# A norm weight that arrives as eight rows and is applied behind the transposes, and an inverse root computed on GpSimd

## The chip, the cores and the metric

The program runs on one core of one Trainium2 chip. A core has five engines with a queue of instructions each: TensorE (PE, with its weight loads listed as PEld), VectorE (DVE), ScalarE (ACT), GpSimd (POOL) and SyncE (SP), which here only starts DMAs. Data moves between HBM and the on-chip memory SBUF by 16 DMA engines; TensorE writes into a second on-chip memory, PSUM, which VectorE and ScalarE can read. The metric is the device time of one execution in microseconds (us); lower is better. Rows with SPq, POOLq or PEq show a queue's own work, such as the issue of a DMA.

## The reference, cut to what matters

All tensors are float32; there are 256 tokens of width 1024. The work is two transformer layers after one another:

```
# first layer
h = rms_norm(x, norm_mix);  z = h @ w_in          # 1024 -> 2560: gated unit, differential attention
x = x + concat(sgu(z), diff_attention(z)) @ w_out
x = x + memory_attention(rms_norm(x, norm_xq), rms_norm(mem, norm_mem), ...)
x = x + hierarchical_moe(rms_norm(x, norm_ffn), ...)   # 32 experts, 2 per token
x = rms_norm(x, norm_final)
# second layer
u = moba_attention(rms_norm(x, norm_mix_pre), w_qkv, w_o)     # 8 heads, all 256 tokens in one block
x = x + rms_norm(u, norm_mix_post)
u = square(relu(rms_norm(x, norm_ffn_pre) @ w_up)) @ w_down   # 1024 -> 4096 -> 1024
out = x + rms_norm(u, norm_ffn_post)

def rms_norm(x, g):
    return x * rsqrt(mean(x * x) + 1e-6) * g       # mean over the 1024 columns of a token
```

Two places matter. The first is the first norm: `norm_mix` is a weight per column, the inverse root a number per token. The second is the border of the layers: the final norm of the first layer and the first norm of the second follow each other, so for each token two inverse roots are needed, `r4[:, 0:2]` for the final norm of the two blocks of 128 tokens and `r4[:, 2:4]` for the norm behind it.

## The kernel before, in words

Matrix products are made nearly exact in float32 by splitting each operand into two parts of a faster 32-bit type, a high part (`hi`, `xh`, `whi`) and the rest (`lo`, `xl`, `wlo`), and adding three products: high with high, high with low, low with high (`mm3`, lines 177 to 179). A weight matrix comes in pieces of 512 columns (`Chunk`, line 102): four quarters of 128x1024 numbers each in `raw` tiles, started on SyncE's queue. For each quarter ScalarE makes the high part (line 129, `whi`) and VectorE subtracts it from the raw numbers for the low part (line 137, `wlo`, an instruction that reads two SBUF tiles). `whi` and `wlo` have six buffers each, `raw` has six of 1 MB.

The start is written out by hand in `first_mixers`, in a `manual_schedule` block: each engine runs its instructions in the order of the code. Before the first product TensorE multiplies the identity with itself (`keep_warm`, line 409: eleven times at first, eight times later), which computes nothing that is used. `norm_mix` is read from HBM 128 times over, once per partition, into a 512 KB tile `gmix` in one of the two buffers named `gb`. VectorE multiplies x by it (lines 424 and 429, one line for each block of 128 tokens), TensorE turns the result (line 387), ScalarE copies the turned block from PSUM as the high part (line 389) and VectorE takes the low part from PSUM (line 394). `project` (line 400) then multiplies by the first 512 columns of `w_in`. The inverse root of the norm is left out of all this and applied later. The `gb` buffers go round: an integer table in `setup` (line 314, read by the VectorE cast of line 318), then `gmix`, then `gmem` (`norm_mem`, line 419), then `norm_xq` (line 217, started on GpSimd's queue).

At the border of the layers (end of `moe`, lines 1292 to 1315) the products with the second layer's weights have already begun: the norms' inverse roots are applied behind the products. `vs` collects four columns, two per block of tokens (lines 1309 to 1312). `rsqrt(k, vs, 4)` makes `r4` with a chain of eight VectorE instructions of four columns (lines 67 and 87 to 94). Here Tile's scheduler orders the instructions, and it has put splits (`wlo`) between the links of this chain. `r4` is wanted by VectorE (`x`, line 1433), by ScalarE for the attention values (line 1455) and by TensorE, which turns it into a row (line 1445); VectorE copies that row to `rb` (line 1446) and scales the queries and keys of the first two heads by it (`by_token`, line 1449), after which TensorE computes their scores (lines 1469 and 1470). On GpSimd the product `gmg` of two weights (line 1505) waits for its second weight's DMA (line 217, `norm_ffn_pre`).

Of the kernel before, what the change touches and what calls it, by code (L numbers as in the profile page):

```python
# [9 lines left out]
F32 = mybir.dt.float32  # L10
# [4 lines left out]
AF = mybir.ActivationFunctionType  # L15
OP = mybir.AluOpType
# [38 lines left out]
def bcast_rows(ap, n):  # L55

    return bass.AP(tensor=ap.tensor, offset=ap.offset, ap=[[0, 128], [1, n]])
# [5 lines left out]
def rsqrt(k, v, n, scale=None):  # L63

    nc = k.nc
    seed = small(k, n, "rqi", dt=I32)
    nc.vector.tensor_scalar(seed, v.bitcast(I32), -0.5, MAGIC, op0=OP.mult, op1=OP.add)
    r0 = seed.bitcast(F32)
    y, w, u = small(k, n, "rqy"), small(k, n, "rqw"), small(k, n, "rqu")
    r = small(k, n, "rqr", 6)  # L70
    if n == 1:
        nc.vector.scalar_tensor_tensor(y, r0, v, r0, op0=OP.mult, op1=OP.mult)
        nc.vector.tensor_scalar(w, y, -1.0, None, op0=OP.add)
        nc.vector.tensor_scalar(u, y, C4, C3 - C4, op0=OP.mult, op1=OP.add)
        t = small(k, 1, "rqt")
        nc.vector.tensor_scalar(t, u, w, C2, op0=OP.mult, op1=OP.add)
        rw = small(k, 1, "rqx")
        if scale is not None:
            rs = small(k, 1, "rqs")
            nc.vector.tensor_mul(rs, r0, scale)  # L80
            r0 = rs
        nc.vector.tensor_mul(rw, r0, w)
        t2 = small(k, 1, "rqt")
        nc.vector.tensor_scalar(t2, t, w, C1, op0=OP.mult, op1=OP.add)
        nc.vector.tensor_scalar(r, t2, rw, r0, op0=OP.mult, op1=OP.add)
        return r
    nc.vector.tensor_mul(y, r0, r0)
    nc.vector.tensor_mul(y, y, v)
    nc.vector.tensor_scalar(w, y, -1.0, None, op0=OP.add)
    nc.vector.tensor_scalar(u, w, C4, C3, op0=OP.mult, op1=OP.add)  # L90
    nc.vector.tensor_mul(u, u, w)
    nc.vector.scalar_tensor_tensor(u, u, C2, w, op0=OP.add, op1=OP.mult)
    nc.vector.scalar_tensor_tensor(u, u, C1, w, op0=OP.add, op1=OP.mult)
    nc.vector.scalar_tensor_tensor(r, u, 1.0, r0, op0=OP.add, op1=OP.mult)
    return r
# [55 lines left out]
def cols(w, c0):  # L151

    return w[:, c0:c0 + 512].rearrange("(kt p) n -> p kt n", p=128)
# [12 lines left out]
def tok(tb):  # L166
    return slice(tb * 128, tb * 128 + 128)


def half(n):  # L170
    return slice(n * 512, n * 512 + 512)
# [49 lines left out]
def small(k, n, name, bufs=4, dt=F32):  # L221
    return k.sm.tile([128, n], dt, name=name if n <= 2 else name + "8", bufs=bufs if n <= 2 else 2)
# [80 lines left out]
def setup(k, const):  # L303
    nc, I = k.nc, k.I
    x = k.new_x().rearrange("p (t n) -> p t n", t=2)
    k.x = x

    ident = const.tile([128, 128], F32, name="ident")
    nc.gpsimd.memset(ident, 1.0)
    nc.gpsimd.affine_select(ident, ident, pattern=[[-1, 128]], compare_op=OP.is_equal, fill=0.0,  # L310
                            base=0, channel_multiplier=1)
    k.ident = ident

    di = k.pa.tile([128, 384], I32, name="gb", bufs=2)
    nc.gpsimd.iota(di[:, 0:128], pattern=[[1, 128]], base=0, channel_multiplier=-1)
    nc.gpsimd.iota(di[:, 128:384], pattern=[[1, 256]], base=-128, channel_multiplier=-1)
    dn = const.tile([128, 384], F32, name="dn")
    nc.vector.tensor_copy(dn, di)
    for c0 in (0, 256):
        nc.gpsimd.affine_select(dn[:, c0:c0 + 128], dn[:, c0:c0 + 128], pattern=[[-1, 128]],  # L320
                                compare_op=OP.is_ge, fill=NEG, base=0, channel_multiplier=1)
    k.dn = dn
# [23 lines left out]
def first_mixers(k):  # L346

    nc, tc, I = k.nc, k.tc, k.I
    x = k.x
    with ExitStack() as ctx:  # L350
        pb = ctx.enter_context(tc.tile_pool(name="pb", bufs=1))
# [15 lines left out]

        wi = I["w_in"][0]
        hT = new_T(k, 0)
        y = k.pa.tile([128, 2, 1024], F32, name="big8", bufs=1)  # L370
        gmix = k.pa.tile([128, 1024], F32, name="gb", bufs=2)
        nc.sync.dma_start(x[:, 0], I["x"][0, tok(0), :])
        nc.sync.dma_start(gmix, bcast_rows(I["norm_mix"], 1024))
        c = Chunk(k, cols(wi, 512), split=False,
                  between=lambda i: i or nc.sync.dma_start(x[:, 1], I["x"][0, tok(1), :]))
        c1, c2 = (Chunk(k, cols(wi, n), split=False) for n in (1024, 1536))
# [2 lines left out]
        xh, xl = hT  # L379
# [3 lines left out]
        def turned(tb, n):  # L383

            pt = k.wk.tile([128, 4, 128], F32, name="wk")
            for j in range(4):
                nc.tensor.transpose(pt[:, j], y[:, tb, tok(4 * n + j)], k.ident)
            d = (slice(None), slice(4 * n, 4 * n + 4), tok(tb))
            nc.scalar.activation(xh[d], pt, AF.Copy)
            return d, pt  # L390

        def lows(todo):
            for d, pt in todo:
                nc.vector.tensor_sub(xl[d], pt, xh[d].bitcast(F32))

        def project(tb, units, passes):

# [8 lines left out]
        def keep_warm(n):  # L406

            for i in range(n):
                nc.tensor.matmul(warm, k.ident, k.ident, start=True, stop=True)
# [9 lines left out]
        nc.sync.dma_start(gmem, bcast_rows(I["norm_mem"], 1024))  # L419
        with tc.manual_schedule(engines={nc.tensor.engine, nc.scalar.engine, nc.vector.engine,  # L420
                                         nc.gpsimd.engine}):
            keep_warm(11)
            for n in range(2):
                nc.vector.tensor_mul(y[:, 0, half(n)], x[:, 0, half(n)], gmix[:, half(n)])
            todo = [turned(0, n) for n in range(2)]
            c.high()
            lows(todo)
            for n in range(2):
                nc.vector.tensor_mul(y[:, 1, half(n)], x[:, 1, half(n)], gmix[:, half(n)])
            keep_warm(8)  # L430
            project(0, range(2), (0, 2))
            c.low(nc.vector)
# [1 line left out]
            todo = [turned(1, n) for n in range(2)]  # L434
# [46 lines left out]
            for i in range(8):  # L481
                tb, g = divmod(i, 4)
# [80 lines left out]
        for i in range(8):  # L563
            tb, g = divmod(i, 4)
# [47 lines left out]
        for qb in range(2):  # L612
            o = t2([128, 4, 128])
# [27 lines left out]
        for qb in range(2):  # L641
            o = os[qb]
            nc.vector.tensor_mul(o, o, ro[:, qb * 4:qb * 4 + 4, None].to_broadcast([128, 4, 128]))
            pt = k.wk.tile([128, 4, 128], F32, name="wk")
# [14 lines left out]
        y, parts = project_add(k, (mh, ml), I["w_out"][0], gxq)  # L659
# [273 lines left out]
def moe(k, oT):  # L933
# [3 lines left out]
    nc, tc, I = k.nc, k.tc, k.I  # L937
    x = k.x
    wg, wu, wd = I["w_gate"][0], I["w_up"][0], I["w_down"][0]
    R = Routing()  # L940
    with ExitStack() as ctx:
# [9 lines left out]
        y = R.raw2.tile([128, 2048], F32, name="raw").rearrange("p (t n) -> p t n", t=2)  # L951
# [157 lines left out]
        def keep_warm(tb, n):  # L1109

            for i in range(n):
                nc.tensor.matmul(macc[tb][0][:, 0:128], k.ident, k.ident, start=True, stop=True)
# [8 lines left out]
        pool = nc.gpsimd  # L1121
# [156 lines left out]
        with tc.manual_schedule(engines=order_of):  # L1278
            for p in range(SPILL, NP - 2):
                if p == GAINS:  # L1280
                    gains.extend(load_gain(k, name, nc.sync) for name in ("norm_final", "norm_mix_pre_2"))
                pair(p)
            gf, g1 = gains
            pool.tensor_tensor(g1, g1, gf, op=OP.mult)
            last_pairs()
            hT = new_T(k, 0)
            scatter(*pend, last=True)
            gained_T(k, R, macc, gains[1], hT, ahead[0])
            for i in range(2):
                ahead[1].high()  # L1290
                ahead[1].low()
            first = token_major(k, hT, ahead[0], range(8), pool=k.wk)
            x = k.x = k.new_x().rearrange("p (t n) -> p t n", t=2)
            y = k.pa.tile([128, 2, 1024], F32, name="big8", bufs=1)
            vs = small(k, 4, "vs")
            for tb in range(2):
                px, py = [], []
                for n in range(2):
                    xs, ys = x[:, tb, half(n)], y[:, tb, half(n)]
                    nc.vector.tensor_mul(ys, macc[tb][n], gf[:, half(n)])  # L1300
                    px.append(mean_sq(k, macc[tb][n], xs))
                    if n == 0:
                        py.append(mean_sq(k, ys, xs))
                    else:
                        py.append(small(k, 1, "ms", 8))
                        nc.vector.scalar_tensor_tensor(xs, ys, 1.0 / 1024, ys, op0=OP.mult, op1=OP.mult,
                                                       accum_out=py[n])
                v1, v2 = vs[:, tb:tb + 1], vs[:, 2 + tb:3 + tb]
                nc.vector.tensor_scalar(v1, px[0], px[1], RMS_EPS, op0=OP.add, op1=OP.add)
                my = small(k, 1, "my")  # L1310
                nc.vector.tensor_add(my, py[0], py[1])
                nc.vector.tensor_scalar(v2, v1, RMS_EPS, my, op0=OP.mult, op1=OP.add)
                ahead[1].high()
                ahead[1].low(nc.vector)
            r4 = rsqrt(k, vs, 4)
    return hT, ahead, first, y, r4


# [401 lines left out]
```

## Time and profile before

| | us |
|---|---|
| median of 3 runs (990.01 to 991.66) | 991.53 |
| the profiled execution, its time | 991.24 |
| its span, first to last instruction | 989.3 |
| TensorE busy in the span | 937.9 (95%) |
| VectorE busy | 450.0 (45%) |
| ScalarE busy | 329.2 (33%) |
| GpSimd busy | 39.8 (4%) |

The span is what the rows show; 1.94 us of the execution's time lie around it. The granted TensorE clock was 0.992 of full speed on average. TensorE is nearly always busy, but not everywhere on work that sets the end: between about 240 and 684 us, in the experts' stage, the weights stream in at some 420 GB/s and TensorE waits for them here and there. A busy share therefore says little; which wait ends last, stage by stage, says more.

### The profile page before, as it was taken

Reading aid. Unit: us, or ns where it says so; the run is one execution under the profiler, and the core shown is the slowest. Engines: PE = TensorE matmul, PEld = TensorE weight load, DVE = VectorE, ACT = ScalarE, POOL = GpSimd, SP = SyncE. Lnnn points to the kernel's source line nnn. Section 1 sums busy time; section 2 is a strip of 40 time slices with the busy share of each in tenths; the row PEclk is TensorE's granted clock in tenths of the full one; section 3 lists DMA queues with packets and bytes.
Section 4 is the critical chain, followed back from the end, with each engine's and each line's share of the span. In section 5 each row is a group of like instructions: output and inputs, shape, how many; then the busy total and the mean of one; then the engine's idle time right before and its main releaser. Section 6 shows DMA issues by size and latency. Waiting matters only on the chain. (4 is left out here: it accounts for less than half of the span.)

```text
span 989.3 us, 13343 instructions
## 1 busy us (share of the span) xinstructions
PE 937.9 (95%) x5308; PEld 650.5 (66%) x5308; DVE 450.0 (45%) x852; ACT 329.2 (33%) x518; POOL 39.8 (4%) x41
## 2 busy tenths in 40 slices
PE   8999999999999999999989999898999999999996
PEld 7988899874344444444334444334889879999995
DVE  6798775653221211111121211015875687555554
ACT  6657555531110110111111101103554455445541
POOL 0030000230000000000000000000120000000000
PEclk9999999999999999999999999999999999999999
DMA  9955464697999999999999999999845346655501
GB/s 355 353 205 177 140 211 137 201 348 279 401 426 421 424 421 424 425 422 424 423 420 413 421 424 422 423 424 400 291 149 171 128 152 196 205 174 196 185 1 43
DMA packets 86576, 293.23 MB, mean 296 GB/s; under 512 B 7088, under 2 KB 15824, under 8 KB 73712
## 3 DMA queue, kind: packets, MB, share of 16 engines
q1 hardware_dynamic: 85616, 289.56, 75.7%
q0 software_dynamic: 896, 2.79, 0.8%
q8 instruction: 43, 0.70, 0.3%
q14 instruction: 21, 0.17, 0.0%
HBM read 291.28 MB, written 1.05 MB: 295 GB/s over the span
## 5 line engine op out<-in xcount | busy, mean ns | idle before, releaser
L137 DVE TENSOR_TENSOR wlo<-raw,whi 128x1024 fp32r<-128x1024 f32 x156 | 189.0, 1222 | 100.4 <-ACT whi L129 99.4
L129 ACT ACTIVATE whi<-raw 128x1024 fp32r<-128x1024 f32 x156 | 163.0, 1057 | 143.7 <-PE acc L179 59.7
L1236 DVE COPY usb<-wk 128x512 f32<-128x512 f32 x16 | 11.0, 689 | 201.9 <-PE wk L1074 183.6
L177 PE MATMUL acc<-hTh,whi 128*128 128x256 f32 x352 | 101.3, 288 | 0.0
L179 PE MATMUL acc<-hTh,wlo 128*128 128x256 f32 x352 | 100.9, 287 | 0.0
L178 PE MATMUL acc<-hTl,whi 128*128 128x256 f32 x352 | 100.7, 286 | 0.0
L1074 PE MATMUL wk<-raw,hTh 128*64 128x512 f32 x272 | 82.8, 614 | 7.3 <-DMA raw<-in_w_up 4.4
L1197 PE MATMUL wk<-raw,v 128*64 128x512 f32 x216 | 67.5, 594 | 9.9 <-issue 8.5
L1210 ACT ACTIVATE hTl<-wk,wc 128x512 fp32r<-128x512 f32 x32 | 22.0, 687 | 164.6 <-PE wk L1197 164.5
L177 PEld LDWEIGHTS acc<-hTh,whi 128*128 128x128 f32 x352 | 68.2, 194 | 1.2 <-issue 1.0
L178 PEld LDWEIGHTS acc<-hTl,whi 128*128 128x128 f32 x352 | 68.2, 194 | 0.2
L179 PEld LDWEIGHTS acc<-hTh,wlo 128*128 128x128 f32 x352 | 68.2, 194 | 0.1
L1074 PE MATMUL wk<-raw,hTl 128*64 128x512 f32 x208 | 67.4, 594 | 0.0
L1211 DVE SCALAR_TENSOR_TENSOR hTl<-wk,wc,hTl 128x512 fp32r<-128x512 f32 x32 | 24.0, 751 | 94.9 <-ACT hTl L1210 93.1
L177 PE MATMUL wk<-hTh,whi 128*128 128x256 f32 x224 | 63.5, 284 | 0.0
L179 PE MATMUL wk<-hTh,wlo 128*128 128x256 f32 x224 | 63.4, 283 | 0.0
L178 PE MATMUL wk<-hTl,whi 128*128 128x256 f32 x224 | 63.4, 283 | 0.0
L179 PE MATMUL acc<-whi,hTl 128*128 128x512 f32 x160 | 63.2, 395 | 0.0
L177 PE MATMUL acc<-whi,hTh 128*128 128x512 f32 x160 | 63.1, 396 | 0.0
L178 PE MATMUL acc<-wlo,hTh 128*128 128x512 f32 x160 | 62.9, 393 | 0.0
L1074 PEld LDWEIGHTS wk<-raw,hTh 128*64 128x64 f32 x272 | 26.1, 141 | 50.3 <-issue 39.4
L178 PE MATMUL acc<-wlo,a 128*128 128x512 f32 x128 | 49.9, 390 | 0.0
(417 smaller groups left out, 1694.9 us busy)
## 6 DMA issues: line engine op xcount, KB each, us to landing
raw<-in_w_up SPq DMA_DIRECT2D x47, 1024.0 KB, 8.5
raw<-in_w_down SPq DMA_DIRECT2D x45, 1024.0 KB, 11.2
raw<-in_w_gate SPq DMA_DIRECT2D x29, 1024.0 KB, 14.7
whi<-in_w_down SPq DMA_DIRECT2D x25, 512.0 KB, 11.0
wlo<-in_w_down SPq DMA_DIRECT2D x25, 512.0 KB, 10.2
whi<-in_w_gate SPq DMA_DIRECT2D x23, 512.0 KB, 11.1
wlo<-in_w_gate SPq DMA_DIRECT2D x23, 512.0 KB, 9.9
whi<-in_w_up SPq DMA_DIRECT2D x22, 512.0 KB, 12.1
```

What stands on the lines that cost most here:

```text
L129: self.k.nc.scalar.activation(hi, self.quarter(len(self.his)), AF.Copy)
L137: (eng or k.nc.vector).tensor_tensor(lo, self.quarter(i), self.his[i].bitcast(F32), op=OP.subtract)
L177: nc.tensor.matmul(out, lh, rh, start=start, stop=False, skip_group_check=True)
L178: nc.tensor.matmul(out, lh, rl, start=False, stop=False, skip_group_check=True)
L179: nc.tensor.matmul(out, ll, rh, start=False, stop=stop, skip_group_check=True)
L1074: nc.tensor.matmul(ps[side(i)], xg[:, 2 * (p % 2) + i], w[:, half(kt % 2)], start=(kt == 0), stop=(kt == 7), tile_position=(0, 64 * i), sk ...
L1197: nc.tensor.matmul(py[n][side(i)], v[:, f, side(i)], w[:, half(n)], start=(f == 0), stop=(f == 3), tile_position=(0, 64 * i), skip_group_c ...
L1210: nc.scalar.activation(yh[:, s], py[n], AF.Copy, scale=R.wc[:, p:p + 1])
L1211: nc.vector.scalar_tensor_tensor(yl[:, s], py[n], R.wc[:, p:p + 1], yh[:, s].bitcast(F32), op0=OP.mult, op1=OP.subtract)
L1236: nc.vector.tensor_copy(u, ps)
```

## The change

The first part replaces the 512 KB load of `norm_mix` by one of 8 rows of 128 numbers (4 KB) on ScalarE's queue, into `grow`. TensorE turns it into a 128x8 tile, from which VectorE copies `gmix`. x itself is turned, without its weight; VectorE multiplies the turned block in PSUM by `gmix` (in this layout the weight is a number per partition and block of columns) into `z`, and high and low part come from `z` in SBUF. `keep_warm(11)` becomes `keep_warm(7)`. The second part replaces the eight VectorE instructions of `rsqrt(k, vs, 4)` by one GpSimd instruction that raises `vs` to the power -0.5.

```diff
+    k.mhalf = const.tile([128, 1], F32, name="mhalf")
+    nc.gpsimd.memset(k.mhalf, -0.5)
...
-        y = k.pa.tile([128, 2, 1024], F32, name="big8", bufs=1)
-        gmix = k.pa.tile([128, 1024], F32, name="gb", bufs=2)
+        y = k.pa.tile([128, 2, 2, 4, 128], F32, name="big8", bufs=1)
+        grow = pb.tile([8, 128], F32, name="grow")
+        nc.scalar.dma_start(grow, I["norm_mix"].rearrange("o (kt p) -> (o kt) p", p=128))
         nc.sync.dma_start(x[:, 0], I["x"][0, tok(0), :])
-        nc.sync.dma_start(gmix, bcast_rows(I["norm_mix"], 1024))
...
             for j in range(4):
-                nc.tensor.transpose(pt[:, j], y[:, tb, tok(4 * n + j)], k.ident)
+                nc.tensor.transpose(pt[:, j], x[:, tb, tok(4 * n + j)], k.ident)
+            z = y[:, tb, n]
+            nc.vector.tensor_tensor(z, pt, gmix[:, 4 * n:4 * n + 4, None].to_broadcast([128, 4, 128]), op=OP.mult)
             d = (slice(None), slice(4 * n, 4 * n + 4), tok(tb))
-            nc.scalar.activation(xh[d], pt, AF.Copy)
-            return d, pt
+            nc.scalar.activation(xh[d], z, AF.Copy)
+            return d, z
...
-            keep_warm(11)
-            for n in range(2):
-                nc.vector.tensor_mul(y[:, 0, half(n)], x[:, 0, half(n)], gmix[:, half(n)])
+            keep_warm(7)
+            gt = k.wk.tile([128, 8], F32, name="wk")
+            nc.tensor.transpose(gt, grow, k.ident[0:8, 0:8])
+            gmix = pb.tile([128, 8], F32, name="gmix")
+            nc.vector.tensor_copy(gmix, gt)
             todo = [turned(0, n) for n in range(2)]
             c.high()
             lows(todo)
-            for n in range(2):
-                nc.vector.tensor_mul(y[:, 1, half(n)], x[:, 1, half(n)], gmix[:, half(n)])
             keep_warm(8)
...
-            r4 = rsqrt(k, vs, 4)
+            r4 = small(k, 4, "rqr", 6)
+            pool.tensor_tensor(r4, vs, k.mhalf.to_broadcast([128, 4]), op=OP.pow)
```

VectorE's order at the start of the program, before the change (`big` is the weighted x, `hTl` its low part):

```order
L424 TENSOR_TENSOR big_100<-x,gb 128x512 x2
L318 CAST dn<-gb 128x384
L394 TENSOR_TENSOR hTl_99<-wk,hTh 128x4x128 x2
L429 TENSOR_TENSOR big_100<-x,gb 128x512 x2
L137 TENSOR_TENSOR wlo<-raw,whi 128x1024 x2
L394 TENSOR_TENSOR hTl_99<-wk,hTh 128x4x128 x2
```

The same stretch of VectorE's order with the change (`big` is now `z`, the turned and weighted block):

```order
L320 CAST dn<-gb 128x384
L430 COPY gmix<-wk 128x8
L391 TENSOR_TENSOR big_102<-wk,gmix 128x512 x2
L398 TENSOR_TENSOR hTl_101<-big_102,hTh 128x4x128 x2
L137 TENSOR_TENSOR wlo<-raw,whi 128x1024
L391 TENSOR_TENSOR big_102<-wk,gmix 128x512 x2
L137 TENSOR_TENSOR wlo<-raw,whi 128x1024
L398 TENSOR_TENSOR hTl_101<-big_102,hTh 128x4x128 x2
```

The weighting moves behind the transposes, and the second block's weighting now stands between the first two splits of the weights instead of ahead of both. The cast of the integer table, which frees the first `gb` buffer, now comes first of all.

VectorE's order at the border of the layers, before the change (from the last column of `vs` to the scaling of queries and keys):

```order
L1312 TENSOR_SCALAR vs_5274<-vs_5274,my 128x1
L137 TENSOR_TENSOR wlo<-raw,whi 128x1024
L67 TENSOR_SCALAR rqi_5311<-vs_5274 128x4
L137 TENSOR_TENSOR wlo<-raw,whi 128x1024
L87 TENSOR_TENSOR rqy_5313<-rqi_5311 128x4
...
L89 TENSOR_SCALAR rqw_5314<-rqy_5313 128x4
...
L94 SCALAR_TENSOR_TENSOR rqr_5316<-rqu_5315,rqi_5311 128x4
L1433 TENSOR_SCALAR x<-big_5273,rqr_5316 128x1024 x2
L1446 COPY rb<-wk 128x256
L137 TENSOR_TENSOR wlo<-raw,whi 128x1024
L1449 SCALAR_TENSOR_TENSOR a_5344<-acc,rb 128x512 x2
```

The same stretch of VectorE's order with the change (line 1438 is the former 1433, 1454 the former 1449):

```order
L1316 TENSOR_SCALAR vs_5276<-vs_5276,my 128x1
L137 TENSOR_TENSOR wlo<-raw,whi 128x1024
L1438 TENSOR_SCALAR x<-big_5275,rqr_5313 128x1024 x2
L137 TENSOR_TENSOR wlo<-raw,whi 128x1024 x4
L1451 COPY rb<-wk 128x256
L137 TENSOR_TENSOR wlo<-raw,whi 128x1024
L1454 SCALAR_TENSOR_TENSOR a_5334<-acc,rb 128x512 x2
```

Six splits stood between `vs` and the row copy, now five; the scaling of x, which waits for `r4`, moved ahead of four of them. One split follows the copy in both.

GpSimd's order at the border of the layers with the change (the power is line 1320, `gmg` line 1510; without line 1320 it is also the order before):

```order
L217 DMA gb<-in_norm_mix_post 128x1024
L217 DMA gb<-in_norm_ffn_pre 128x1024
L1320 TENSOR_TENSOR rqr_5313<-vs_5276,mhalf 128x4
L1510 TENSOR_TENSOR gmg<-gb 128x1024
```

The power stands ahead of `gmg`. On TensorE the turning of `r4` into a row stood behind four products of the next weight piece; it now stands twelve products before the end of the piece in hand, and the scores stand 32 products behind it.

## Rows read from the trace of the kernel before

**Rows 1.** Chain of work that ended last, one piece (start us, us, what)
```profile
538.82 15.90 DMA whi<-in_w_down
```

**Rows 2.** Busy time by stretch: length, engines' busy time, clock, DMA share, GB/s
```profile
5.00:10.00 5.00, 3.47 (x30) 3.10 (x29) 2.88 (x6) 1.95 (x3) 0.54 (x2) 1.00 0.98 378
...
230.00:240.00 10.00, 10.00 (x55) 4.60 (x55) 2.87 (x6) 1.56 (x3) 0.00 (x0) 1.00 0.45 164
380.00:420.00 40.00, 37.15 (x186) 18.01 (x184) 8.63 (x16) 3.76 (x6) 0.00 (x0) 1.00 1.02 423
```

**Rows 3.** TensorE's waits: us in total, times, longest
```profile
PE acc L552 <- ACT t L550: 1.4, 1, 1.4
PE wk L1445 <- DVE rqr L94: 2.3, 1, 2.3
```

**Rows 4.** Timeline of the start: start us, us, instruction, [idle before, what ended it]
```profile
0.81 0.39 SPq L372 DMA_DIRECT2D x<-in_x  x1
...
1.60 4.23 PE L409 MATMUL wk<-ident 128*128 128x128 f32 x22 [1.60 <-POOL ident L310]
1.73 0.43 SPq L110 DMA_DIRECT2D raw<-in_w_in  x1
...
6.61 1.29 DVE L424 TENSOR_TENSOR big<-x,gb 128x512 f32<-128x512 f32 x2 [6.61 <-DMA gb<-in_norm_mix]
...
7.36 1.26 PE L387 MATMUL wk<-ident,big 128*128 128x128 f32 x8 [1.53 <-DVE big L424]
...
8.05 1.20 ACT L389 ACTIVATE hTh<-wk 128x512 fp32r<-128x512 f32 x2 [5.96 <-PE wk L387]
...
9.14 1.05 ACT L129 ACTIVATE whi<-raw 128x1024 fp32r<-128x1024 f32 x1
...
10.42 1.06 ACT L129 ACTIVATE whi<-raw 128x1024 fp32r<-128x1024 f32 x1 [0.23 <-DMA raw<-in_w_in]
...
11.09 2.36 DVE L137 TENSOR_TENSOR wlo<-raw,whi 128x1024 fp32r<-128x1024 f32 x2
...
14.32 1.07 PE L400 MATMUL acc<-whi,hTh 128*128 128x512 f32 x4
```

**Rows 5.** Line 372, the load of x's first block, issue to landing
```profile
DMA to landing us min/median/max: 3.5/3.5/3.5
```

**Rows 6.** Line 110, the first two weight quarters, issue to landing
```profile
DMA to landing us min/median/max: 6.1/6.9/7.7
```

**Rows 7.** Timeline of VectorE at the border of the layers
```profile
704.08 0.21 DVE L1312 TENSOR_SCALAR vs<-vs,my 128x1 f32<-128x1 f32 x1
704.21 1.22 DVE L137 TENSOR_TENSOR wlo<-raw,whi 128x1024 fp32r<-128x1024 f32 x1
...
708.97 2.39 DVE L89 TENSOR_SCALAR rqw<-rqy 128x4 f32<-128x4 f32 x1
...
714.39 1.42 DVE L1433 TENSOR_SCALAR x<-big,rqr 128x1024 f32<-128x1024 f32 x2
...
717.19 1.28 DVE L1449 SCALAR_TENSOR_TENSOR a<-acc,rb 128x512 f32<-128x512 f32 x2
```

**Rows 8.** Timeline of GpSimd at the border of the layers
```profile
707.95 3.38 POOL L1505 TENSOR_TENSOR gmg<-gb 128x1024 f32<-128x1024 f32 x1 [5.45 <-ACT whi L129]
```

**Rows 9.** Timeline of TensorE ahead of its wait at line 1445
```profile
711.54 0.28 PE L177 MATMUL acc<-hTh,whi 128*128 128x256 f32 x1
711.66 0.28 PE L178 MATMUL acc<-hTl,whi 128*128 128x256 f32 x1
```

**Rows 10.** Busy time by stretch, behind that wait
```profile
715.00:718.00 3.00, 3.00 (x16) 3.00 (x16) 3.00 (x6) 0.70 (x2) 0.00 (x0) 0.50 0.67 238
```

**Rows 11.** Timeline of GpSimd in the first layer
```profile
54.48 1.36 POOL L569 TENSOR_TENSOR a<-a,lng 128x512 f32<-128x512 f32 x1 [15.16 <-ACT whi L129]
...
57.71 5.57 POOL L569 TENSOR_TENSOR a<-a,lng 128x512 f32<-128x512 f32 x1 [0.49 <-DVE a L566]
```

**Rows 12.** Timeline of VectorE in the same stretch
```profile
57.48 4.62 DVE L137 TENSOR_TENSOR wlo<-raw,whi 128x1024 fp32r<-128x1024 f32 x4
```

More of the change, by code (lines that the diff above doesn't have):

```diff
@@ L386, in turned @@
             for j in range(4):
-                nc.tensor.transpose(pt[:, j], y[:, tb, tok(4 * n + j)], k.ident)
+                nc.tensor.transpose(pt[:, j], x[:, tb, tok(4 * n + j)], k.ident)
+            z = y[:, tb, n]
+            nc.vector.tensor_tensor(z, pt, gmix[:, 4 * n:4 * n + 4, None].to_broadcast([128, 4, 128]), op=OP.mult)
             d = (slice(None), slice(4 * n, 4 * n + 4), tok(tb))
-            nc.scalar.activation(xh[d], pt, AF.Copy)
-            return d, pt
+            nc.scalar.activation(xh[d], z, AF.Copy)
+            return d, z
         def lows(todo):
-            for d, pt in todo:
-                nc.vector.tensor_sub(xl[d], pt, xh[d].bitcast(F32))
+            for d, z in todo:
+                nc.vector.tensor_sub(xl[d], z, xh[d].bitcast(F32))
         def project(tb, units, passes):
```

## The prediction

> **What bounds the kernel now.** I read the chain of waits first. Its long pieces lie between 538 and 684 us and are transfers of expert weights [rows 1]; the table by stretch says the same, with 423 GB/s from 380 to 420 us [rows 2]. That stream is no anchor in time, though: between 230 and 240 us it ran at 164 GB/s [rows 2], because its buffers were still held by TensorE's work. So the stream starts when the work ahead of it allows, and what is saved at the program's start is passed on to the end. Behind the stream TensorE sets the pace. TensorE's waits come next: behind 705 us its largest is 2.3 us at line 1445, for the last link of the inverse-root chain; in the first layer one of 1.4 us stands at line 552 [rows 3]. The timelines of both places give the rest.
>
> **The start.** Before, VectorE began at 6.61 us, when the 512 KB weight landed [rows 4]; x's first block was there at 0.81 + 3.5 = 4.3 [rows 4, 5]. With the change the transposes need x, and for the tiny transpose ahead of them the 4 KB of `grow`. No row shows so small a load at the start. It is bounded by the first load's 3.5 us and, from above, by the 7.7 of the slower weight quarter [rows 5, 6]; I take 3.5, since it is the first on a queue of its own. The seven warm-up products end at 1.60 + 7 x 4.23/11 = 4.3 [rows 4], so nothing is late by them. Step by step, with durations of rows 4: eight transposes 1.26, to 5.7; a weighting is 0.65, so the two end at 6.4; the high copies 0.60 each, to 7.0; the low parts 1.29, to 8.3. The first weight quarter landed between 1.73 + 6.1 = 7.8 before [rows 4, 6] and 1.24 earlier (512 KB at 423 GB/s, rows 2) at best. From 7.8, its high copy (1.05) ends at 8.9 instead of 10.2, its low part (1.18, half of 2.36) at 10.1.
>
> Then the new order costs something: the second block's two weightings (1.29) stand ahead of the second split, so VectorE is free for it at 11.4. Its high copy waited for a transfer until 10.42 before; it ends between 10.3 and 11.5. The second split so ends at 12.3 to 12.7, where it ended at 13.45. Two products later (0.27 each at most) TensorE begins the second block, at 12.7 to 13.2 instead of 14.32 [rows 4]. From there to line 552 TensorE has no wait of note [rows 3], so the gain here is 1.1 to 1.6; I take 1.4. The freed transfer is worth less than its size, because another one takes its place: the first `gb` buffer is freed by the cast, which now comes first, so the load of `norm_xq` (512 KB, GpSimd's queue), which stood behind line 429, leaves some 8 us earlier, into the same crowded stretch. That is why I count none of the 1.24 in full. If `grow` lands 7.7 us after its issue, the transposes start at 8.5, later than the 7.36 of before, and the gain turns into a loss of about 1.
>
> At line 552, products that wait for ScalarE stand three products earlier in TensorE's order than before. The wait's end is not TensorE's to set, so three products of 0.12 [rows 9] move behind it: a loss of 0.4.
>
> **The border of the layers.** Removed are eight small VectorE instructions. Seven cost 0.1 to 0.2 each; line 89 took 2.39 [rows 7], and that is not its own: it ended when GpSimd's `gmg` did, at 707.95 + 3.38 = 711.33 [rows 8]. Both rows together show that the engines shut each other out: `gmg` got going when a split ended (708.97) and then needed 2.36, while VectorE stood. The other direction is plainer. Line 569 takes 1.36 alone and took 5.57 under four splits in a row (57.48 to 62.10), and it ended 1.2 behind them [rows 11, 12]. So a split holds GpSimd's two-input instruction off, and splits without a gap hold it off together.
>
> For the power that means: `vs` is complete at 704.29, but the split behind it runs until 705.43 [rows 7], and the power waits for that. Its own cost p shows in no row. Nearest below is VectorE's instruction on `vs`, 0.21 [rows 7], nearest above GpSimd's product of 512 columns, 1.36 [rows 11]; if each of four columns cost as much as that product, 5.4. I take 0.8, between the near ones. Behind it, in VectorE's new order: two scalings of x 1.42, four splits 4.62, the row copy and one split 1.38 (715.81 to 717.19), the scaling of queries and keys 1.28 [rows 7, 12]. `gmg`, ready at 707.95, is held off by the four splits, starts with the copy, and holds the split behind it for 2.36 - 0.3 = 2.0. The sum: 705.43 + 0.8 + 1.42 + 4.62 + 1.38 + 2.0 + 1.28 = 716.9, when the scores can start.
>
> TensorE no longer waits for `r4`: the turn stands at about 710, when the power is long done. From 711.54 [rows 9] it has the two turns (moved from behind) and 20 products at 0.12, to 714.2; then the scores, which wait until 716.9. So the old wait of 2.3 is replaced by one of 2.7 some two microseconds later: a loss of 0.4. The old one had a second price, a granted clock of 0.50 (1.2 instead of 2.4 GHz) from 715 to 718 [rows 10], about 1.5 us of work. An idle time of 1.53 at the start left the clock at 1.00 [rows 2, 4], the one of 2.3 did not; 2.7 will pay it again, so nothing is gained there. VectorE's saved instructions are hidden by that wait. ScalarE's value copies now stand ahead of three high copies, whose splits stand behind others on VectorE anyway: nothing.
>
> Here a rule of the Trainium skill speaks against the change ("SBUF — State Buffer", section "Who interferes with whom"): a VectorE instruction with two inputs in SBUF and a GpSimd instruction that reads SBUF exclude each other for the whole instruction. The trace agrees, with 5.57 us against 1.36. With it the sum is the one above; without it, the one of the first rival below.
>
> Sum against the profiled execution, 991.24: 991.24 - 1.4 + 0.4 + 0.4 = 990.6. The median of the runs shown is 991.53, 0.3 above that execution.
>
> **The rivals.** (1) `gmg` doesn't stand in the way of the scores: it slips in where VectorE waits for the power, or goes last. For it speaks that the scaling of queries and keys reads PSUM beside one SBUF tile; against it that `gmg` becomes ready in the midst of the splits. The scores then start at 714.9, TensorE idles 0.7 instead of 2.3 and keeps its clock: 1.6 + 1.5 saved instead of 0.4 lost, 990.6 - 3.5 = 987.1. If only the clock stays, 989.1.
>
> (2) The start gains nothing: the change doesn't free the transfer, since `norm_xq` comes in its place. For it: the two loads have one size and the early stretch is full; against it: x's first block already landed 2.3 us ahead of the weight. If the second quarter comes 1.24 later than before, its split ends at 13.9 and the second block starts at 14.3, as before: 990.6 + 1.4 = 992.0.
>
> (3) Slower: the power is dear. One instruction, line 1320, holds up VectorE, which waits for it at the scaling of x with all later splits queued behind, and so TensorE. Every microsecond over 0.8 is one at the end. At 5.4, 990.6 + 4.6 = 995.2; it is slower by more than can be told from p = 3.4. For it: a power isn't a product, and no row shows one. Against it: the columns are four.
>
> The skill has a rule for this case ("GPSIMD Engine Reference", section "Instruction dispatch"): the first call of a freshly loaded routine costs about 6 us that no instruction shows. By that the estimate is near 996; no run here shows a power, and the first two-input product on GpSimd, 1.36 at 54.48, shows no such price.
>
> **How the numbers follow.** Forecast 0.50, rival 1 0.20, rival 2 0.14, rival 3 0.16. What a measurement of this kernel can tell from no change is 0.2%, 2.0 us, so the bounds are 989.2 and 993.2. The forecast's own range, with the start between -0.5 and 1.6 and p between 0.2 and 1.4 nearly certain, is 989.5 to 992.9; 0.05 of it may lie below and 0.03 above the bounds. Rival 1 is faster but for 0.01, rival 2 the same but for 0.02, rival 3 slower but for 0.01. Faster 0.05 + 0.19 = 0.24; slower 0.03 + 0.02 + 0.15 = 0.20; the same 0.56. The range reaches to the full gain of rival 1 (987.0) and leaves out the greater part of rival 3: 987.0 to 993.6.
>
> **What the profile would show.** Right: the first transposes near 4.5 us, the second block's products near 13; line 1320 starting at about 705.4 (less the shift of the start) with VectorE idle until its end; `gmg` long, and the split behind the row copy ending late; a wait of TensorE of two to three microseconds at the scores, and half the clock behind it. Wrong would be: transposes that wait for `grow`; a power of several microseconds; no wait at the scores, or a clock of 1.00 throughout that stretch.

## The result, and the profile after

The changed kernel took 1000.55 us (median of 5 runs, 1000.01 to 1002.65) beside 991.53 for the kernel before on the same chip: a ratio of 1.0097, 95% interval 1.0085 to 1.0109. 990.6 was forecast, with 993.6 as the upper end: the prediction was wrong, and in sign.

The timelines of VectorE (start us, us, engine, line, operation) give the place: the first weighting behind the experts, which opens the border of the layers, in the kernel before and then in the changed one.

```profile
695.43 1.28 DVE L1300 TENSOR_TENSOR big<-acc,gb 128x512 f32<-128x512 f32 x2
```

```profile
704.06 1.28 DVE L1304 TENSOR_TENSOR big<-acc,gb 128x512 f32<-128x512 f32 x2
```

It comes 8.6 us later. The experts' weights are loaded from 156 us on, ahead of their use; the load below, one of the last before the long stream, is issued by SP's queue at the same time in both, before and after.

```profile
221.79 0.33 SPq L1016 DMA_DIRECT2D raw<-in_w_gate  x1
```

```profile
221.84 0.33 SPq L1020 DMA_DIRECT2D raw<-in_w_gate  x1
```

So neither of the two edited places holds the main loss; it lies between them, where the diff changes no instruction. This row of the changed kernel's table by stretch answers to [rows 2] (length, busy time of PE, PEld, DVE, ACT, POOL, clock, DMA share, GB/s).

```profile
380.00:420.00 40.00, 37.15 (x188) 17.98 (x186) 8.63 (x16) 3.76 (x6) 0.00 (x0) 1.00 1.02 414
```

From 380 to 420 the DMA engines are as busy as before (1.02) and move 414 GB/s instead of 423 [rows 2], with the same work on every other engine. A stage of 474 us (from that load to the weighting), most of it bound by the stream, lengthened by 2.1% would be 10 us longer; 8.6 are missing.

The start, in the changed kernel's timeline, answers to [rows 4].

```profile
2.98 0.70 POOL L217 DMA_DIRECT2D gb<-in_norm_xq  x1
8.10 1.04 ACT L129 ACTIVATE whi<-raw 128x1024 fp32r<-128x1024 f32 x1
...
10.39 1.06 ACT L129 ACTIVATE whi<-raw 128x1024 fp32r<-128x1024 f32 x1 [1.25 <-DMA raw<-in_w_in]
...
12.07 1.22 DVE L137 TENSOR_TENSOR wlo<-raw,whi 128x1024 fp32r<-128x1024 f32 x1
...
13.91 1.09 PE L404 MATMUL acc<-whi,hTh 128*128 128x512 f32 x4
```

The second block's products begin 0.4 earlier, not 1.4: the second weight quarter lands no sooner than before (10.42 in [rows 4]). TensorE's waits answer to [rows 3].

```profile
PE acc L556 <- ACT t L554: 1.8, 1, 1.8
PE wk L1474 <- DVE a L1454: 3.0, 1, 3.0
```

Both are as forecast: 1.4 became 1.8, and in place of the wait for the inverse root stands one at the scores. The timeline of VectorE and GpSimd at the border answers to [rows 7, 8]; line 1320 is the power.

```profile
712.72 0.21 DVE L1316 TENSOR_SCALAR vs<-vs,my 128x1 f32<-128x1 f32 x1
712.85 1.21 DVE L137 TENSOR_TENSOR wlo<-raw,whi 128x1024 fp32r<-128x1024 f32 x1
713.02 1.95 POOL L1320 TENSOR_TENSOR rqr<-vs,mhalf 128x4 f32<-128x4 f32 x1 [1.89 <-DVE vs L1316]
715.01 1.42 DVE L1438 TENSOR_SCALAR x<-big,rqr 128x1024 f32<-128x1024 f32 x2 [0.94 <-POOL rqr L1320]
...
715.80 2.89 POOL L1510 TENSOR_TENSOR gmg<-gb 128x1024 f32<-128x1024 f32 x1 [0.83 <-ACT a L1460]
...
716.34 6.85 DVE L137 TENSOR_TENSOR wlo<-raw,whi 128x1024 fp32r<-128x1024 f32 x4
723.11 0.41 DVE L1451 COPY rb<-wk 128x256 f32<-128x256 f32 x1
...
724.57 1.28 DVE L1454 SCALAR_TENSOR_TENSOR a<-acc,rb 128x512 f32<-128x512 f32 x2
```

The power starts under a split and ends 0.9 behind it. The four splits take 6.85 instead of 4.62, because `gmg` stands among them.

### The profile page after: what moved, and what is told of

The parts are those of the page before. It is cut to its first block, busy times and chain, and to the rows that moved or that the text cites. A ratio compares the mean times of both kernels' runs of the same rounds, so it can differ in the third digit from the quotient of the medians.

```text
span 998.8 us, 13319 instructions
## 1 busy us (share of the span) xinstructions
PE 942.1 (94%) x5301; PEld 650.9 (65%) x5301; DVE 449.8 (45%) x844; ACT 329.4 (33%) x518; POOL 40.8 (4%) x43
## 5 line engine op out<-in xcount | busy, mean ns | idle before, releaser
L137 DVE TENSOR_TENSOR wlo<-raw,whi 128x1024 fp32r<-128x1024 f32 x156 | 191.5, 1240 | 100.5 <-ACT whi L129 98.4
L1233 ACT ACTIVATE sg<-wk 128x512 f32<-128x512 f32 x16 | 9.6, 598 | 122.7 <-PE wk L1184 122.7
```

Of the source, the lines that this page charges most:

```text
L137: (eng or k.nc.vector).tensor_tensor(lo, self.quarter(i), self.his[i].bitcast(F32), op=OP.subtract)
L1233: nc.scalar.activation(sg, pt, AF.Silu)
```

## The experiments

One thing in the diff reaches the experts' stage. The new tile `mhalf`, one column, takes 32 bytes a partition in the program's first pool, so every later tile of the built program lies 32 bytes higher: the raw buffers at 21,536 + 8,192 k bytes, where they were at 21,504 + 8,192 k, a multiple of 512. Theory A: the stream is slower because its destinations start elsewhere. Rivals: B, the new queue on ScalarE; C, the new order at the start or the border.

**The shift alone** (the kernel before, with an unused tile).

```
     k.ident = ident
+    k.pad = const.tile([128, 1], F32, name="mhalf")   # 1: 32 bytes; 16, 32, 64 columns below
+    nc.gpsimd.memset(k.pad, -0.5)
```

> The kernel before with one thing more: an unused constant tile of 32 bytes a partition in the first pool, in the place that the change gives its tile mhalf, written once by GpSimd. In the built program every later tile lies 32 bytes higher (the raw buffers at 21,536 + 8,192 k bytes instead of 21,504 + 8,192 k). Theory A, that the weights' stream slows because its destinations no longer start on a multiple of 64 bytes: all of the 8.6 us lost in the experts' stage comes back here without any edit of the change, 1000 us (998 to 1001), and the stream reads 414 GB/s instead of 423 in the window from 380 to 420. Theory B, that ScalarE's new DMA queue slows the others: there is none here, 991.5, 423 GB/s. Theory C, that the new order at the start or at the border slows the stream: 991.5 too.

998.17 us, 1.0069 [1.0052, 1.0086]. None of the change is in it, and the rate falls just so; this is its row by stretch, TensorE's work the same to the hundredth.

```profile
380.00:420.00 40.00, 37.15 (x188) 17.99 (x184) 8.63 (x16) 3.77 (x6) 0.00 (x0) 1.00 1.02 414
```

TensorE's equal work in this row does not speak against the stream. The stream runs ahead of TensorE, which is late only when that lead is used up: the load issued at 473.24 us before is issued at 478.57 here, 5.3 later, while the products of line 1197 (1199 here) are 0.7 late at 472 and 7.8 late at 563. These are their rows, before and then here.

```profile
472.03 0.61 PE L1197 MATMUL wk<-hTh,v 128*64 128x512 f32 x1 [1.42 <-issue]
562.82 1.92 PE L1197 MATMUL wk<-whi,v 128*64 128x512 f32 x8
```

```profile
472.71 0.61 PE L1199 MATMUL wk<-hTh,v 128*64 128x512 f32 x1 [1.43 <-issue]
570.60 1.92 PE L1199 MATMUL wk<-whi,v 128*64 128x512 f32 x8
```

That shows A: the shift by itself makes most of the loss. B and C could add to it, not explain it.

**The change with a larger tile**: `mhalf` of 16 columns, a shift of 64 bytes.

> The changed kernel with its tile mhalf enlarged from 32 to 64 bytes a partition, so that every later tile starts on a multiple of 64 bytes again (the raw buffers at 21,568 + 8,192 k). All edits of the change stay. Theory A (alignment of the stream's destinations): 423 GB/s again, and what is left is the change itself: its start gains 0.4, the later wait loses 0.4, the border loses 0.9, so 992.4 us (991 to 993.5). Theories B (ScalarE's queue) and C (the order): 1000, 414 GB/s.

1000.01 us, 1.0092 [1.0075, 1.0109], 416 GB/s. The expectation failed: 64 is no better a step.

**The change without ScalarE's queue**: `nc.scalar.dma_start(grow, ...)` becomes `nc.sync.dma_start(grow, ...)`.

> The changed kernel with the load of the eight rows of the norm's weight issued on SP's queue instead of ScalarE's, so that the program has no third queue of issued DMAs. The 32-byte shift of the tiles stays. Theory A (alignment): 1000 us (999 to 1002), 414 GB/s. Theory B (a further queue slows the stream): 992, 423 GB/s. Theory C (the order): 1000.

1000.6 us, 1.0101 [1.0081, 1.0121], 414 GB/s (300 to 460). B falls.

**The kernel before, shifted by 64, 128 and 256 bytes.**

> The kernel before with an unused constant tile of 64 bytes a partition in the first pool: the same added instruction and a shift of all later tiles by 64 bytes. Theory A (starts on a multiple of 64 bytes are what matters): 991.5 us (991 to 992), 423 GB/s. A variant of it, that a start on a multiple of 512 bytes is what matters (the raw buffers lie at such starts before and no longer do here): 1000, 414 GB/s. Theories B and C: 991.5.

> The kernel before with an unused constant tile of 128 bytes a partition in the first pool. A shift of 256 bytes cost nothing, one of 64 bytes 6 us. If a start on a multiple of 128 bytes is enough: 991.5 us, 423 GB/s. If it must be a multiple of 256: 997 us (996 to 998.5), 416 to 417 GB/s.

> The kernel before with an unused constant tile of 256 bytes a partition in the first pool, so that the raw, whi and wlo buffers start 256 bytes off a multiple of 512. If only a start on a multiple of 512 bytes is fast (theory A'): 998 us (996 to 1000), 415 or 416 GB/s. If a multiple of 256 is enough: 991.5 us, 423 GB/s. If the price falls with the part of a 512-byte piece that is left over, by the runs so far (414 GB/s at 32 bytes off, 416 at 64): 418 to 420 GB/s, 994 to 996 us.

64: 997.78 us, 1.0065 [1.0048, 1.0082], 416 GB/s. 128: 998.78, 1.0078 [1.0062, 1.0093], 415. 256: 991.56, 1.0002 [0.9993, 1.0011], with this row by stretch.

```profile
380.00:420.00 40.00, 37.15 (x188) 17.99 (x186) 8.63 (x16) 3.76 (x6) 0.00 (x0) 1.00 1.02 423
```

Of these starts, those on a multiple of 256 bytes are the fast ones. Off it, the price is about the same at 32, 64 and 128: a step, not a slope. It also settles that the added memset is free.

**The change without its tile.** The exponent goes into the power's own result.

```
-    k.mhalf = const.tile([128, 1], F32, name="mhalf")
-    nc.gpsimd.memset(k.mhalf, -0.5)
...
-            pool.tensor_tensor(r4, vs, k.mhalf.to_broadcast([128, 4]), op=OP.pow)
+            pool.memset(r4, -0.5)
+            pool.tensor_tensor(r4, vs, r4, op=OP.pow)
```

> The changed kernel without its constant tile: the exponent -0.5 is written by a memset into the power's own result tile, which the power then reads and overwrites. All edits of the change stay, and every tile that the experts' stage uses lies at the byte where it lies in the kernel before (the raw buffers at 21,504 + 8,192 k). Theory A', that the stream slows because the shift took its destinations off their starts on a multiple of 512 bytes: 423 GB/s from 380 to 420, and what is left is the change itself, 0.4 gained at the start, 0.4 lost at the later wait and 0.9 at the border: 992.4 us (991 to 993.5). Theory C, that the new order at the start or at the border slows the stream: 1000, 414 GB/s.

992.9 us, 1.0017 [1.0008, 1.0026], 423 GB/s. With every edit in place and no tile moved, 0.80% of the 0.97% are back (1.0097 - 1.0017). C falls, and A is shown from both sides.

**Which destinations.** The 32 bytes are put in between the raw buffers and those behind them.

```
+    gap = ctx.enter_context(tc.tile_pool(name="gap", bufs=1))
+    k.pad = gap.tile([128, 1], F32, name="gap")
+    k.nc.gpsimd.memset(k.pad, -0.5)
     k.whi = ctx.enter_context(
```

> The kernel before with an unused tile of 32 bytes a partition between the pool of the six raw buffers and that of whi: raw stays at 21,504 + 8,192 k, and whi, wlo and everything above lie 32 bytes higher. Theory A' (each transfer is slowed by its own destination's start): the loads into whi, wlo, x, gb, hTh and hm are slowed, the six raw buffers' are not; by the page's counts that is about half of the stream's bytes (70 loads of 512 KB into each of whi and wlo and some 25 MB into others, of about 190 MB), so about half of the 6.7 us of a shift of everything: 994.6 us (993.5 to 996), 418 to 419 GB/s from 380 to 420. If only the split buffers that the engines write matter, or one shifted buffer slows all the others: 998. If only the raw buffers matter: 991.5.

996.8 us, 1.0050 [1.0034, 1.0065], 418 GB/s. The rate fell by half as much as with the full shift, as the bytes say; the time rose by 5 us of the 6.8 of the full shift, more than expected, though the intervals overlap. The rows of SP's queue show which loads pay. In these stretches each issue waits for a landing (from 378.5 to 388.4 here the profile gives four waits for `raw<-in_w_gate`, 8.2 us in all), so two issues span the loads that land between them: in the first fence of each pair four loads of 1 MB into raw buffers that keep their start here, in the second eleven of 512 KB into `whi` and `wlo`. The kernel before:

```profile
376.60 0.33 SPq L1016 DMA_DIRECT2D wlo<-in_w_up  x1
386.40 0.33 SPq L1016 DMA_DIRECT2D wlo<-in_w_up  x1
```

```profile
344.37 0.33 SPq L1016 DMA_DIRECT2D wlo<-in_w_gate  x1
358.01 0.33 SPq L1016 DMA_DIRECT2D hTh<-in_w_down  x1
```

This kernel:

```profile
378.55 0.33 SPq L1016 DMA_DIRECT2D wlo<-in_w_up  x1
388.32 0.33 SPq L1016 DMA_DIRECT2D wlo<-in_w_up  x1
```

```profile
345.82 0.33 SPq L1016 DMA_DIRECT2D wlo<-in_w_gate  x1
359.83 0.33 SPq L1016 DMA_DIRECT2D hTh<-in_w_down  x1
```

The raw loads take 9.77 instead of 9.80, nothing lost; those into `whi` and `wlo` take 14.01 instead of 13.64. With everything shifted (the shift alone) the same loads take 9.99 and 14.03. So each load pays for its own start, and both kinds pay 2 to 3%.

**The last two buffers.** Two raw buffers of the experts' stage lie 192 above a multiple of 256 in the kernel before. A tile of 64 bytes, never written, moves them.

```
         nc.vector.tensor_copy(R.flag, ff)
+        R.gap = R.mp.tile([128, 16], F32, name="gap")
```

> The kernel before with one tile of 64 bytes, never written, as the last of the experts' stage's own pool: no instruction is added, and the two raw buffers of that stage, which the kernel before has at 212,672 and 220,864 bytes (192 above a multiple of 256), start at 212,736 and 220,928, on multiples of 256. Theory A': these two of eight raw buffers took some 30 of the stream's 190 MB at the slow rate, so 16% of what a shift of everything costs (6.3 us) comes back: 990.4 us (989.8 to 991), and 424 GB/s. If a start off a multiple of 256 costs only where all buffers have it: 991.4.

990.73 us, 0.9994 [0.9985, 1.0003]: the expected 1 us lies within the interval, and so does nothing. In the traces the loads into these two buffers land 2.47 us behind the load ahead of them in the kernel before and 2.45 here (medians of 16, between 290 and 660 us). So 192 bytes off cost about 0.02 us a load, less than the 0.05 of 32 off (2.50, the shift alone), and some 30 such loads had, by this estimate, 0.6 us to give.

**The start alone**, without tile and power; then with the load of `norm_xq` held back.

```
             todo = [turned(1, n) for n in range(2)]
+            gxq = k.pa.tile([128, 1024], F32, name="gb", bufs=2)
+            nc.gpsimd.tensor_copy(gxq[:, 0:1], todo[1][1][:, 0, 0:1])
+            nc.gpsimd.dma_start(gxq, bcast_rows(I["norm_xq"], 1024))
...
-        gxq = load_gain(k, "norm_xq")
```

> The start's part alone: eight rows of the weight, applied at the transposes' copy-out, with the Newton iteration at the border and no new constant tile. Theory A': 423 GB/s, and the two small effects at the program's start cancel: 991.5 us (990.8 to 992.3). Theory C, with the start as what slows the stream: 999.

> The start's part alone, with the load of the memory attention's norm weight (512 KB on GpSimd's queue, issued at 2.93 where the start's part is made, at 11.48 before) held back behind the second block's copy-outs by a one-element copy of GpSimd that reads them. Theory S, that this load took the place of the weight's load that the change removes: the second quarter of the first weight chunk lands at about 9.2 instead of 10.4, the second block's products begin at 12.7 to 13.2 instead of 13.8, and 1 us is gained against the start's part alone: 990.6 us (989.8 to 991.4). Rival, that the quarter's own queue sets its landing: products at 13.8, 991.5 us.

991.65 us, 1.0005 [0.9994, 1.0015], and 991.21, 0.9996 [0.9984, 1.0008]. The timeline of the second:

```profile
8.87 1.06 ACT L129 ACTIVATE whi<-raw 128x1024 fp32r<-128x1024 f32 x1 [0.24 <-DMA raw<-in_w_in]
...
11.55 1.22 DVE L137 TENSOR_TENSOR wlo<-raw,whi 128x1024 fp32r<-128x1024 f32 x1
...
12.82 0.73 PE L402 MATMUL acc<-wlo,hTh 128*128 128x512 f32 x2 [0.68 <-DVE wlo L137]
...
13.39 1.09 PE L402 MATMUL acc<-whi,hTh 128*128 128x512 f32 x4
```

Theory S is right on the transfer: held back, `norm_xq` lets the second quarter in by 8.87, where it came at 10.36 in the start alone. It is wrong on the gain: the products begin at 13.39, and at 13.31 in the start alone (13.8 was expected there, from the changed kernel). VectorE, which has the second block's weightings ahead of the split and waits for the transposes with them, is late in the transfer's place.

**The border alone**, with the power as in the change without its tile.

> The border's part alone: the four-column inverse root as a power on GpSimd, its exponent written into its result tile, so that no tile moves; the start as before. Theory A': 423 GB/s and a loss at the border of 0.9 us, as the changed kernel's trace has it: 992.4 us (991.8 to 993.2). Theory D, that the power itself costs more than it seems: 994 or later, with the loss behind 695 us in the trace.

992.1 us, 1.0012 [1.0003, 1.0021]. Theory D falls: the scaling that waits for the power starts 0.94 behind the split here too. VectorE's timeline shows what is late.

```profile
704.27 0.21 DVE L1312 TENSOR_SCALAR vs<-vs,my 128x1 f32<-128x1 f32 x1
704.40 1.22 DVE L137 TENSOR_TENSOR wlo<-raw,whi 128x1024 fp32r<-128x1024 f32 x1
706.56 3.58 DVE L1435 TENSOR_SCALAR x<-big,rqr 128x1024 f32<-128x1024 f32 x2 [0.94 <-POOL rqr L1317]
710.06 4.62 DVE L137 TENSOR_TENSOR wlo<-raw,whi 128x1024 fp32r<-128x1024 f32 x4
...
716.07 1.27 DVE L1451 SCALAR_TENSOR_TENSOR a<-acc,rb 128x512 f32<-128x512 f32 x2
```

The two scalings took 3.58 where they took 1.42 in [rows 7]: `gmg`, started at 706.90, held them up. **The same with `gmg` held back** behind the second product `xg`:

```
+        nc.gpsimd.tensor_copy(gmg[:, 0:1], xg[1][:, 0:1])
         nc.gpsimd.tensor_tensor(gmg, gm, g2, op=OP.mult)
```

> The border's part alone, with the product gmg on GpSimd held behind the two products xg (it is first read at 788 us) by a one-element copy that reads the second of them; the orders of TensorE and VectorE stay. Theory G, that gmg holds VectorE's scaling of x back (3.58 us in the border's part alone, where two such scalings take 2.67) and with it all that follows to the attention's scores: the scaling takes 2.7, TensorE's wait at the scores shrinks from 2.2 to about 1.3 and 0.9 us comes back: 991.2 us (990.5 to 991.9). Rival P, that the loss is the power's own 0.94 of VectorE's idle time and TensorE's order alone: 992.1 us.

989.7 us, 0.9990 [0.9980, 1.0001], 2.2 us (0.22%) better than the border alone by the two ratios. Its timeline:

```profile
703.88 0.21 DVE L1312 TENSOR_SCALAR vs<-vs,my 128x1 f32<-128x1 f32 x1
704.01 1.22 DVE L137 TENSOR_TENSOR wlo<-raw,whi 128x1024 fp32r<-128x1024 f32 x1
706.17 1.42 DVE L1435 TENSOR_SCALAR x<-big,rqr 128x1024 f32<-128x1024 f32 x2 [0.95 <-POOL rqr L1317]
707.50 4.62 DVE L137 TENSOR_TENSOR wlo<-raw,whi 128x1024 fp32r<-128x1024 f32 x4
...
713.51 1.28 DVE L1451 SCALAR_TENSOR_TENSOR a<-acc,rb 128x512 f32<-128x512 f32 x2
```

From `vs` to the scaling `a`: 9.6 us, against 11.8 with `gmg` there and 13.1 before [rows 7]. TensorE's wait at the scores is gone, which is more than theory G expected (it had `gmg` cost 0.9; it cost 2.2), and the clock stays at 1.00. P falls.

**Together.** Start held back and the two buffers moved; then also the power with `gmg` held back.

> Start's part with the norm weight's load held back, and the two raw buffers of the experts' stage moved by 64 bytes onto multiples of 256; the border as before (Newton). If both small gains are real and add up (0.2 and 0.7 by the medians of their own runs): 990.4 us (989.8 to 991.2). If both were noise: 991.4.

> As the kernel of the line before, with the power at the border and gmg held behind xg. By theory G the border then costs 0 to 0.3 against the Newton iteration: 990.6 us (989.8 to 991.5). By theory P it costs 1.2: 991.6.

991.3 us, 1.0006 [0.9997, 1.0015]: the interval leaves out the 0.9 us that the two would give together, so the small gains were noise. And 989.36, 0.9991 [0.9982, 0.9999]: about 1 us faster than the kernel before, with an interval that ends just below 1. One such interval among fifteen kernels would be weak by itself; the border alone with `gmg` held back gives the same 1 us (0.9990), and the kernel with the start and the buffers alone nothing, so what there is comes from the border.

## Why the prediction was wrong

**The step that failed** is the first: "So the stream starts when the work ahead of it allows", with the rate of 423 GB/s [rows 2] carried over unchanged into the sum. Only the start of the stage was asked after, not its rate. A tile of one column was costed at nothing by not being costed at all; it took 8.6 us at 704.06. None of the rivals had it. In its place the runs show a stream of 414 GB/s at the same DMA share, slowed by the start of its destinations alone: the shift without any edit of the change makes 0.69% of the 0.97%. The Trainium skill ("DMA: Bandwidth & Descriptors", section "How a descriptor splits into AXI transactions") has the rule that would have warned: a transfer is cut into pieces of 256 bytes that start on multiples of 256, so a row of whole pieces that starts elsewhere needs one more. The runs agree on 256. The Trainium skill says it there of what is read, and counts the bytes fetched in vain, by which 128 off should cost four times what 32 off does; the runs show it of what is written, at one price (415 and 414 GB/s). By the Trainium skill's count of pieces, 33 for 32 in a row of 8,192 bytes and 17 for 16 in one of 4,096, the estimate is 3 to 6%; measured were 2.1% of the rate, and 2 to 3% for either row. What the DMA engines do with such a row, no run here shows.

**The sentence behind it**, that what is saved at the start is passed on, holds only as far as line 552. The start alone brought the second block's products from 14.32 to 13.31, but the wait at line 552 ended only 0.56 earlier, as these rows of TensorE show, before and in the start alone.

```profile
81.82 0.49 PE L552 MATMUL acc<-a,t 128*128 128x128 f32 x2 [1.41 <-ACT t L550]
```

```profile
81.26 0.49 PE L554 MATMUL acc<-a,t 128*128 128x128 f32 x2 [1.77 <-ACT t L552]
```

The three products that now stand behind this wait, 0.12 each, took 0.36 of it; that is the loss of 0.4 that the prediction had as a term of its own. The load of 221.79 was issued at 221.64: of 1.0 us, 0.15 arrived, and the time was that of the kernel before. In the changed kernel, whose start gained 0.4, nothing arrived (221.84).

**The start's term**, 1.4, measured 0.4 in the changed kernel and 1.0 in the start alone. Three more kernels with this start lie between (13.49 to 13.57, against 14.32 to 14.50 in nine with the old one). The changed kernel is the latest: its first eight transposes took 1.52, where the start alone has 1.09; why, no row shows. The warning that `norm_xq` takes the freed place was right (rival 2's mechanism), yet 1.24 of it was still counted in part; and held back it gave the products nothing, since VectorE was not ready. Line 552's loss of 0.4 came as forecast.

**The border's term**: the power was taken at 0.8 and showed 0.9, `gmg`'s hold was taken at 2.0 and was 2.2. The place of that hold was wrong: `gmg` was forecast behind the four splits and got in ahead of them, among the splits or, in the border alone, among the scalings. It costs VectorE the same there, so that the sum came out is partly luck. The scores waited 3.0 instead of 2.7. The loss was taken at 0.4. The clean measure is from the start of the row that completes `vs` (704.08 in [rows 7]) to the second group of score products on TensorE (731.72 in the kernel before). In TensorE's order the same 196 products of the weight piece stand ahead of that group in every kernel, and where TensorE waits between the two ends, the span does not depend on how far it had come at the first; with `gmg` held back it has no such wait, but its products end just as the scaling does (714.84 and 714.79). In this table, "Newton" is the chain of eight VectorE instructions, and "clock fell" means the granted clock behind the wait.

| border | clock fell | us | clock stayed | us |
|---|---|---|---|---|
| Newton | before | 27.6 | start alone, two buffers moved, start with the load held back | 26.1, 26.2, 26.2 |
| power, `gmg` in the way | border alone, change without tile | 28.4, 28.5 | change without ScalarE's queue | 27.3 |
| power, `gmg` held back | | | border with `gmg` held back | 25.1 |

So the power lost 0.8 to 1.2 as the change has it, and gains 1.0 once `gmg` is away: with the power the first group of scores stands 18 products (behind 116 instead of 134, 2.2 us at 0.12) further ahead in TensorE's order, and the scaling `a` came only 1.3 earlier. Rival 1 was the right picture of what lies in this edit, and rival 3 had no part.

With the rate left alone, the measured time would have lain in the range: 992.9, the change without its tile. The sign would still have been wrong: that kernel is 0.17% slower than the one before [0.08, 0.26], where a small gain was forecast, with the start's term too large and the border's loss too small.

## What to carry to other kernels

Where a stage is bound by DMA into SBUF, as the experts' stage is here, a new tile ahead of its buffers is a change of that stage: look where the buffers start before and after, and keep them on a multiple of 256 bytes (put small constants last, in a used tile, or in a slot rounded up to 256). A moved or faster producer helps only if what shares its engine gets out of the way too; the product that nobody needed for 80 us cost twice what the edit could gain (2.2 against 1.0). And ask of every stage that the diff doesn't touch whether its rate, not only its start, is still the same.

## What the runs showed of the hardware

- The start of a DMA's destination in SBUF: 423 GB/s on multiples of 256 bytes, 414 to 416 at 32, 64 or 128 bytes off, at the same DMA share of 1.02 (380 to 420 us). Each load pays for its own start.
- The scaling that waits for a power of 128 x 4 on GpSimd started 0.94 or 0.95 behind the split that held the power, in all seven kernels that have one. The Trainium skill's price of a first call, about 6 us, which the prediction quoted ("GPSIMD Engine Reference", section "Instruction dispatch"), does not show.
- TensorE's clock behind a wait is not decided by the wait's length alone. After waits of 1.4 to 1.8 at the border it stayed at 1.00; after 2.2, 2.9 and 3.0 it fell to its lower level, as in this row of the border alone; after 2.3 it fell in the kernel before and stayed in the start with the load held back. These two have the same wait and spans of 27.6 and 26.2 in the table above, so the fall cost 1.5 us there; by the other pairs it cost 1.1 to 1.5.

```profile
718.00:720.00 2.00, 2.00 (x9) 1.79 (x8) 1.27 (x3) 0.00 (x0) 0.22 (x1) 0.54 1.09 303
```
